# A two-layer hybrid decoder trunk on one core: the first block of the down matrix moved ahead of the last gate and up product, a float32 copy of x made on GpSimd, and constants loaded later

## The chip, the core and the metric

The kernel runs on one core of a Trainium2 chip. A core has TensorE (PE, matrix products into PSUM), VectorE (DVE), ScalarE (ACT), GpSimd (POOL) and SyncE (SP, which issues the large DMAs here). Each engine works through its own instructions in the order in which they stand and waits for the others at semaphores. The metric is the time of one execution on the device in microseconds. The kernel before takes 2764.95 us, the median of three runs (2758.95 to 2766.28).

## The reference

Two layers run over 512 positions of width 1024 in float32. Each layer is a half-step SwiGLU feed-forward network, a mixer of three parallel branches, and a second feed-forward network, with a layer norm behind each:

```
def swiglu(x, w_gate, w_up, w_down):
    return (jax.nn.silu(x @ w_gate) * (x @ w_up)) @ w_down

for l in range(DEPTH):                       # DEPTH = 2
    x = layer_norm(DEEPNORM_ALPHA * x + 0.5 * swiglu(x, ffn1_gate[l], ffn1_up[l], ffn1_down[l]), ln_g[l, 0], ln_b[l, 0])
    mix = token_mixing(x, w_in[l], ...)      # sparse attention, dilated attention, gated MLP; rope tables and masks
    x = layer_norm(DEEPNORM_ALPHA * x + mix, ln_g[l, 1], ln_b[l, 1])
    x = layer_norm(DEEPNORM_ALPHA * x + 0.5 * swiglu(x, ffn2_gate[l], ffn2_up[l], ffn2_down[l]), ln_g[l, 2], ln_b[l, 2])
```

The hidden width is 2816, so gate and up are 1024 x 2816 matrices and down is 2816 x 1024. So there are four feed-forward stages in a run, and the change touches these and nothing in the mixers.

## The kernel before

**Numbers in two parts.** Every operand of TensorE is kept as a high part (rounded to fp32r) and a low part (the rest), and a product is three matmuls: high by high, high by low, low by high (`mm3`, L460 to L462). Making the two parts is a copy on ScalarE and a subtraction on VectorE (or GpSimd). For weights this is `split_w`: L386 the copy into `wh`, L389 the subtraction into `wl`. Weights come by DMA into three `raw` buffers (L424) and are split into eight half buffers, which are handed out again when a product has used them (`put_w`). `pump(look)` splits as many weights ahead as there are free halves.

**Start of a feed-forward stage.** The four row blocks of x (128 positions each) are transposed on TensorE when they are needed (`ensure_x`, `x_transposed`): transposes L534, high part on ScalarE L537, low part on VectorE L540, and a float32 copy `xt` from PSUM on ScalarE L542. From the third block on `x_sums` builds sums of quarters of x out of `xt`: L557 and L559 on VectorE, L558 and L560 on GpSimd, then their two parts (L563, L564). The first two of the 22 column blocks of gate and up are done plainly, first over the positions of blocks 0 and 1, then over those of 2 and 3.

**Gate and up.** For the other 20 blocks (`f`) the product of a 2 x 2 split of x with one of gate and up is done with seven quarter products instead of eight (`A11`, `S1`, `A12`, `S2`, `A22`, `S4`, `S3`; `product`, twelve matmuls of 256 columns each). The sums of weight quarters are made by GpSimd (L407). Results leave PSUM by small copies and additions (L780, L782, L784, L787, L791, L793, L795). `A22` of a block is left for the next block: `end(prev)` runs it behind `S2` of the block that follows, so that it does not have to wait for L795, which reads the same PSUM bank. Behind the last block there is none that follows, and `end(prev)` (L799) comes right behind `S3` and its L795. `product` calls `pump(LOOK)` right behind `put_w`, so the splits of weights stand ahead of the copy out of PSUM on ScalarE and VectorE.

**Down.** `make(n)` splits a 128-row block of the hidden matrix (L808 on ScalarE, L809 on VectorE). Its ten places are taken from an area of 80 blocks (L802), which takes in that of the quarter sums of x, freed behind the last `end` (L800). `tm_gemm` then runs eleven weight blocks for each half of the output columns; a weight block is 24 matmuls of 512 columns, 2 rows of the hidden matrix by 4 row blocks by 3. The first weight block is called block 0 here, and the place where gate and up end and down begins is called the turn.

**Constants.** Rope tables and masks are first used in the mixer. They are loaded by GpSimd's own DMAs in block `f == 4` of the first stage (`load_consts`), and GpSimd turns the masks into bf16 (L509) when they have landed.

## Time and profile before

| | |
|---|---|
| median of three runs | 2764.95 us |
| the profiled execution | 2764.18 us |
| its span, first to last instruction | 2762.5 us |
| TensorE busy | 2630.4 us (95%) |
| VectorE busy | 1769.6 us (64%) |
| ScalarE busy | 1233.1 us (45%) |
| GpSimd busy | 1234.2 us (45%) |
| moved by DMA | 248.72 MB, mean 90 GB/s |

The profiled execution's time lies 1.7 us over its span, and it is 0.8 us under the median. Shares of busy time are means over stages that differ; where a stage is bound is read from the waits of the engine that is never long idle, TensorE. Its busy time holds stretches in which it ran at half its clock, which the page's row PEclk and the stretches below show.

### The profile page before, as it was taken

The page shows a single profiled execution, that of the slowest core. Times are in us where ns is not written, and L with a number is a line of the kernel's source. Part 1 is how long each engine was busy: PE and PEld are TensorE (multiplying, and loading weights), DVE is VectorE, ACT ScalarE, POOL GpSimd, SP SyncE. Part 2 cuts the span into 40 slices and gives each one's busy share as a digit, 9 for nine tenths or more (in the row PEclk, how much of TensorE's full clock was granted, in tenths as well). Part 3 has the DMA queues.
Part 4 walks back from the last instruction along what each step waited for, and adds up shares of the span by engine and source line. Part 5 has one row for each costly group of instructions (what it writes and reads, how often), then busy time and mean ns, then how long its engine had stood idle before and what let it go on. Part 6 is the DMA issues. An engine that isn't in the chain of part 4 may idle for free. (4 is left out here: it accounts for less than half of the span.)

```text
span 2762.5 us, 43188 instructions
## 1 busy us (share of the span) xinstructions
PE 2630.4 (95%) x16446; PEld 2369.3 (86%) x16446; DVE 1769.6 (64%) x3187; ACT 1233.1 (45%) x2442; POOL 1234.2 (45%) x981
## 2 busy tenths in 40 slices
PE   8999999989999999999989999999899999999998
PEld 8998888877788879997889988888777888899977
DVE  7786565557552379884588765655674424788746
ACT  5454334345642235554355543344456422355542
POOL 5663015454655427760067720254446444376500
PEclk9999999999999999999999999999999999999999
DMA  3333223111212332333223333221112123233332
GB/s 137 119 101 115 96 101 99 36 62 47 69 41 90 102 127 93 107 108 101 83 84 101 107 116 96 96 97 51 54 39 76 43 95 117 98 107 108 100 107 77
DMA packets 71216, 248.72 MB, mean 90 GB/s; under 512 B 8016, under 2 KB 10096, under 8 KB 71008
## 3 DMA queue, kind: packets, MB, share of 16 engines
q1 hardware_dynamic: 68832, 238.25, 25.7%
q0 software_dynamic: 2176, 7.71, 0.9%
q8 instruction: 129, 2.11, 0.3%
q14 instruction: 79, 0.65, 0.1%
HBM read 239.64 MB, written 6.29 MB: 89 GB/s over the span
## 5 line engine op out<-in xcount | busy, mean ns | idle before, releaser
L460 PE MATMUL P<-R,wh 128*128 128x256 f32 (+1 forms) x2976 | 905.5, 304 | 44.3 <-DVE Fa L795 17.6
L461 PE MATMUL P<-R,wh 128*128 128x256 f32 (+1 forms) x2976 | 901.5, 303 | 4.4 <-DVE R L540 4.4
L462 PE MATMUL P<-R,wl 128*128 128x256 f32 (+1 forms) x2976 | 900.7, 303 | 0.8 <-POOL wl L389 0.8
L386 ACT CAST wh<-raw 128x1024 fp32r<-128x1024 f32 (+4 forms) x525 | 429.6, 824 | 546.1 <-PE P L462 261.6
L389 POOL TENSOR_TENSOR wl<-raw,wh 128x1024 fp32r<-128x1024 f32 (+4 forms) x159 | 352.2, 2222 | 704.6 <-ACT wh L386 701.1
L460 PEld LDWEIGHTS P<-R,wh 128*128 128x128 f32 x2976 | 576.4, 194 | 69.2 <-DVE Fa L795 18.4
L389 DVE TENSOR_TENSOR wl<-raw,wh 128x512 fp32r<-128x512 f32 (+2 forms) x367 | 402.0, 1098 | 353.3 <-ACT wh L386 352.9
L460 PE MATMUL P<-wh,R 128*128 128x512 f32 (+3 forms) x1600 | 588.0, 367 | 11.9 <-ACT R L808 5.8
L461 PEld LDWEIGHTS P<-R,wh 128*128 128x128 f32 x2976 | 576.8, 194 | 24.5 <-DVE R L540 6.1
L462 PEld LDWEIGHTS P<-R,wl 128*128 128x128 f32 x2976 | 576.8, 194 | 20.5 <-POOL wl L389 1.0
L462 PE MATMUL P<-wh,R 128*128 128x512 f32 (+3 forms) x1600 | 576.8, 360 | 6.1 <-DVE R L540 4.1
L461 PE MATMUL P<-wl,R 128*128 128x512 f32 (+3 forms) x1600 | 576.7, 360 | 4.1 <-POOL wl L389 2.1
L389 DVE TENSOR_TENSOR wl<-Fa,wh 128x512 fp32r<-128x512 f32 x320 | 361.7, 1131 | 117.3 <-ACT wh L386 116.4
L460 PEld LDWEIGHTS P<-wh,R 128*128 128x128 f32 x1600 | 306.4, 191 | 53.0 <-ACT R L808 6.9
L462 PEld LDWEIGHTS P<-wh,R 128*128 128x128 f32 x1600 | 305.9, 191 | 51.3 <-DVE R L540 5.2
L461 PEld LDWEIGHTS P<-wl,R 128*128 128x128 f32 x1600 | 306.9, 192 | 44.4 <-POOL wl L389 2.9
L407 POOL TENSOR_TENSOR Fa<-raw 128x512 f32<-128x512 f32 x160 | 227.7, 1423 | 199.8 <-DMA raw<-in_wts 189.0
L386 ACT CAST wh<-Fa 128x512 fp32r<-128x512 f32 x320 | 197.1, 617 | 158.3 <-PE P L461 85.0
L407 POOL TENSOR_TENSOR Fa<-raw,Fa 128x512 f32<-128x512 f32 x80 | 135.5, 1693 | 1.9 <-DVE wl L389 1.9
L407 POOL TENSOR_TENSOR Fa<-Fa,raw 128x512 f32<-128x512 f32 x80 | 127.5, 1593 | 6.3
L793 ACT ACTIVATE Fa<-Fa 128x512 f32<-128x512 f32 x80 | 50.6, 632 | 154.3 <-DVE Fa L791 154.3
L1635 POOL TENSOR_SCALAR Fa<-Fa,ac,ga 128x128 f32<-128x128 f32 (+3 forms) x128 | 79.3, 630 | 84.1 <-DVE ac L1631 83.7
(222 smaller groups left out, 3151.0 us busy)
## 6 DMA issues: line engine op xcount, KB each, us to landing
raw<-in_wts SPq DMA_DIRECT2D x400, 512.0 KB, 3.3
raw<-in_wts SPq DMA_DIRECT2D x16, 480.0 KB, 3.2
x_sp<-Fa SPq DMA_DIRECT2D x8, 512.0 KB, 5.3
Fa<-x_sp SPq DMA_DIRECT2D x8, 512.0 KB, 5.2
Fa<-in_ln_g POOLq DMA_DIRECT2D x6, 512.0 KB, 5.2
Fa<-in_ln_b POOLq DMA_DIRECT2D x6, 512.0 KB, 5.8
raw<-in_wts SPq DMA_DIRECT2D x8, 320.0 KB, 3.0
Fa<-in_x SPq DMA_DIRECT2D x4, 512.0 KB, 6.4
```

The lines of the kernel that those rows point to most:

```text
L386: nc.scalar.copy(h, r)
L389: (nc.gpsimd if kind == "full" and (self.pool_lo or j == 1) else nc.vector).tensor_tensor(lo, r, hf, op=OP.subtract)
L407: self.nc.gpsimd.tensor_tensor(v, x, y, op=op)
L460: mm(out, lh, rh, start=start, stop=False, skip_group_check=more)
L461: mm(out, lh, rl, start=False, stop=False, skip_group_check=more)
L462: mm(out, ll, rh, start=False, stop=stop, skip_group_check=more)
L793: nc.scalar.activation(st["g"], st["g"], AF.Silu)
L1635: t.nc.gpsimd.tensor_scalar(e, e, rd[:, br:br + 1], t.ga[:, s["i"], c:c + 1], op0=OP.mult, op1=OP.mult)
```

## The change

There are four edits.

1. In `x_transposed` the float32 copy `xt` is no longer copied out of PSUM by ScalarE. GpSimd adds the high and the low part of x, which lie in SBUF, behind the two subtractions of VectorE.
2. `pump(LOOK)` is called behind the copy out of PSUM instead of inside `product`, and not behind `S3` of the last block.
3. The turn: three of the places for split rows of the hidden matrix are taken in a free area before the blocks begin, and the other eight are those of the quarter sums of x. The first three rows are split behind block 20 of gate and up. `end` of the last block is called by `tm_gemm` through `begun`, behind block 0 of down.
4. `load_consts` is called behind that `end` in the first stage.

```diff
--- before.py
+++ after.py
@@ -258,6 +258,7 @@
         self.xh = self.Ra[:, 0:4096].rearrange("p (k t) -> p k t", k=KT)
         self.xl = self.Ra[:, 4096:8192].rearrange("p (k t) -> p k t", k=KT)
         self.xhf = self.Raf[:, 0:4096].rearrange("p (k t) -> p k t", k=KT)
+        self.xlf = self.Raf[:, 4096:8192].rearrange("p (k t) -> p k t", k=KT)
         self.x = self.Fa[:, FB * 128:].rearrange("p (i d) -> p i d", i=NT)
         dram = ctx.enter_context(tc.tile_pool(name="dr", bufs=1, space=bass.MemoryType.DRAM))
         self.x_sp = dram.tile([NT, 128, D], F32, name="x_sp")
@@ -538,9 +539,10 @@
             jobs.append((b, src, ks, ts))
         for b, src, ks, ts in jobs:
             nc.vector.tensor_tensor(self.xl[:, ks, ts], src, self.xhf[:, ks, ts], op=OP.subtract)
-            if ffn:
-                nc.scalar.copy(xt[:, ks, ts], src)
             self.unbank(b)
+        if ffn:
+            for b, src, ks, ts in jobs:
+                nc.gpsimd.tensor_tensor(xt[:, ks, ts], self.xhf[:, ks, ts], self.xlf[:, ks, ts], op=OP.add)
         if spill:
             self.fa.free(FB + i * KT, KT)
         if ffn and i >= 2:
@@ -620,7 +622,7 @@
             self.nc.vector.scalar_tensor_tensor(xs[:, c], xs[:, c], r, b[:, c], op0=OP.mult, op1=OP.add)
 
 
-    def tm_gemm(self, lhs, nk, l, j, last=False, done=lambda k: None):
+    def tm_gemm(self, lhs, nk, l, j, last=False, done=lambda k: None, begun=lambda: None):
 
         pa, g, b = self.ln_params(l, j)
         if j == 0:
@@ -640,6 +642,8 @@
                 self.put_w(w)
                 done(n * 2)
                 done(n * 2 + 1)
+                if h + n == 0:
+                    begun()
             if h == 0:
                 for t in range(NT):
                     self.residual(t, 0, pb[t])
@@ -755,7 +759,6 @@
                 self.mm3(self.P[b][:, :256], wh[:, ks], wl[:, ks], rh[:, k], rl[:, k],
                          k == 0 and not more, k == 3, more)
             self.put_w(w)
-            self.pump(LOOK)
 
         def end(st):
             f, b = st["f"], st["beta"]
@@ -763,8 +766,18 @@
             nc.vector.tensor_tensor(H(f, slice(0, 256)), st["g"][:, :256], self.P[b][:, :256], op=OP.mult)
             self.unbank(b)
             nc.gpsimd.tensor_tensor(H(f, slice(256, 512)), st["g"][:, 256:], st["p"], op=OP.mult)
+            self.pump(LOOK)
             self.fa.free(st["ga"], 4)
             self.fa.free(st["pa"], 2)
+
+        made, used = [0], [0]
+        spare = [self.ra.alloc(8) for _ in range(3)]
+        places = spare + [self.xt_at + n for n in range(0, 64, 8)]
+
+        def make(n):
+            a, v = places[n % len(places)], H(n % NF)
+            self.nc.scalar.copy(self.rv(a, 4), v)
+            self.nc.vector.tensor_tensor(self.rv(a + 4, 4), v, self.rvf(a, 4), op=OP.subtract)
 
         prev = None
         for f in range(PLAIN, NF):
@@ -778,50 +791,54 @@
             P = [self.P[b][:, :256] for b in (beta, gamma, alpha)]
             product(st, A11, beta)
             nc.scalar.copy(g1, P[0])
+            self.pump(LOOK)
             product(st, S1, gamma)
             nc.scalar.copy(p, P[1])
+            self.pump(LOOK)
             product(st, A12, alpha)
             nc.vector.tensor_tensor(g1, P[2], g1, op=OP.add)
             self.unbank(alpha)
+            self.pump(LOOK)
             product(st, S2, beta, True)
             nc.scalar.copy(g2, P[0])
+            self.pump(LOOK)
             if prev:
                 end(prev)
             product(st, S4, gamma, True)
             nc.vector.tensor_tensor(g2, P[1], g2, op=OP.add)
             self.unbank(gamma)
             nc.scalar.activation(st["g"], st["g"], AF.Silu)
+            self.pump(LOOK)
             product(st, S3, beta, True)
             nc.vector.tensor_tensor(p, P[0], p, op=OP.add)
             prev = st
-            if l + j == 0 and f == 4:
-                self.load_consts()
-        end(prev)
-        self.ra.free(self.xt_at, 64)
-
-        base = self.ra.alloc(80)
-        made, used, hs = [0], [0], NT * 2
-
-        def make(n):
-            a = base + n % 10 * 8
-            v = H(n % NF)
-            self.nc.scalar.copy(self.rv(a, 4), v)
-            self.nc.vector.tensor_tensor(self.rv(a + 4, 4), v, self.rvf(a, 4), op=OP.subtract)
+            if f == NF - 2:
+                for n in range(3):
+                    make(n)
+                    made[0] += 1
+            if f < NF - 1:
+                self.pump(LOOK)
 
         def lhs(k):
             n = k if used[0] < NF else NF + k
-            while made[0] < min(max(n + 5, used[0] + 8), used[0] + 10, 2 * NF):
+            while made[0] < min(max(n + 5, used[0] + 8), used[0] + len(places), 2 * NF):
                 make(made[0])
                 made[0] += 1
             assert made[0] > n >= used[0]
-            a = base + n % 10 * 8
+            a = places[n % len(places)]
             return self.rv(a, 4), self.rv(a + 4, 4)
 
         def done(k):
             used[0] += 1
 
-        self.tm_gemm(lhs, NF, l, j, last, done)
-        self.ra.free(base, 80)
+        def begun():
+            end(prev)
+            if l + j == 0:
+                self.load_consts()
+
+        self.tm_gemm(lhs, NF, l, j, last, done, begun)
+        for a in places:
+            self.ra.free(a, 8)
         self.fa.free(more[0][0], (NF - HB // 4) * 4)
```

How the instructions stand. At the end of gate and up, `P7` is the bank of the last block's product and `P4`, `P2`, `P3`, `P1` are those of down. TensorE before goes from the last product (both `S3` and `A22` write P7) to block 0:

```order
L460 MATMUL P7_78<-R_63,wh_69 128x256
L461 MATMUL P7_78<-R_63,wh_69 128x256
L462 MATMUL P7_78<-R_63,wl_70 128x256
L460 MATMUL P4_75<-wh_69,R_63 128x512
L461 MATMUL P4_75<-wl_70,R_63 128x512
L462 MATMUL P4_75<-wh_69,R_63 128x512
```

TensorE now, first the end of `S3` and the begin of block 0, then the end of block 0, `A22` and block 1:

```order
L463 MATMUL P7_78<-R_63,wl_70 128x256
L461 MATMUL P4_75<-wh_69,R_63 128x512
L462 MATMUL P4_75<-wl_70,R_63 128x512
...
L463 MATMUL P1_72<-wh_69,R_63 128x512
L461 MATMUL P7_78<-R_63,wh_69 128x256
L462 MATMUL P7_78<-R_63,wh_69 128x256
L463 MATMUL P7_78<-R_63,wl_70 128x256
...
L463 MATMUL P7_78<-R_63,wl_70 128x256
L461 MATMUL P4_75<-wh_69,R_63 128x512
```

The twelve matmuls of `A22` have moved behind the 24 of block 0.

ScalarE at the same place, before (`wh<-Fa` and `wh<-raw` are splits of weights, 128x512 a quarter and 128x1024 a block of down; `Fa<-P` copies out of PSUM; `R<-H` rows of the hidden matrix):

```order
L793 ACTIVATE Fa<-Fa 128x512
L386 CAST wh<-Fa 128x512
L780 COPY Fa<-P_78 128x256
L782 COPY Fa<-P_76 128x256
L386 CAST wh<-raw 128x1024
L787 COPY Fa<-P_78 128x256
L386 CAST wh<-raw 128x1024
L793 ACTIVATE Fa<-Fa 128x512
L386 CAST wh<-raw 128x1024 x2
L808 CAST R<-H 128x512 x10
```

ScalarE now:

```order
L810 ACTIVATE Fa<-Fa 128x512
L387 CAST wh<-Fa 128x512
L779 CAST R<-H 128x512 x3
L387 CAST wh<-Fa 128x512
L793 COPY Fa<-P_78 128x256
L796 COPY Fa<-P_76 128x256
L387 CAST wh<-raw 128x1024
L803 COPY Fa<-P_78 128x256
L810 ACTIVATE Fa<-Fa 128x512
L387 CAST wh<-raw 128x1024 x2
L779 CAST R<-H 128x512 x5
```

Three splits of the hidden matrix stand a whole block earlier, the last split of a quarter stands behind them, and the second weight block of down is split behind the activation instead of ahead of it.

GpSimd at the start of the second gate and up stage, before (the layer norm's parameters, four subtractions for the first plain weights, the sums of x):

```order
L603 DMA Fa<-in_ln_b 128x1024
L389 TENSOR_TENSOR wl<-raw,wh 128x1024 x4
L558 TENSOR_TENSOR H<-H 128x512
L560 TENSOR_TENSOR H<-H 128x512
L558 TENSOR_TENSOR H<-H 128x512
```

GpSimd now:

```order
L605 DMA Fa<-in_ln_b 128x1024
L545 TENSOR_TENSOR H<-R 128x4x128 x2
L390 TENSOR_TENSOR wl<-raw,wh 128x1024 x3
L545 TENSOR_TENSOR H<-R 128x4x128 x2
L390 TENSOR_TENSOR wl<-raw,wh 128x1024
L545 TENSOR_TENSOR H<-R 128x4x128 x2
L560 TENSOR_TENSOR H<-H 128x512
L562 TENSOR_TENSOR H<-H 128x512
L545 TENSOR_TENSOR H<-R 128x4x128 x2
```

The additions (L545) stand ahead of the subtractions for the first weights and ahead of both sums of x.

## Rows read from the trace of the kernel before

**Rows 1.** The page: busy time by engine, and one group of GpSimd additions.
```profile
PE 2630.4 (95%) x16446; PEld 2369.3 (86%) x16446; DVE 1769.6 (64%) x3187; ACT 1233.1 (45%) x2442; POOL 1234.2 (45%) x981
...
L407 POOL TENSOR_TENSOR Fa<-raw,Fa 128x512 f32<-128x512 f32 x80 | 135.5, 1693 | 1.9 <-DVE wl L389 1.9
```

**Rows 2.** TensorE's waits: waiting line, releaser: us in all, times, longest.
```profile
PE P L460 <- DVE Fa L795: 17.6, 4, 4.4
...
PE P L460 <- ACT Fa L780: 9.1, 11, 1.8
```

**Rows 3.** Timeline of TensorE, first turn: start, us, instruction [idle before <-releaser].
```profile
251.94 0.58 PE L460 MATMUL P<-R,wh 128*128 128x256 f32 x1 [4.41 <-DVE Fa L795]
...
256.31 0.79 PE L460 MATMUL P<-wh,R 128*128 128x512 f32 x1 [1.44 <-ACT R L808]
...
257.98 0.79 PE L462 MATMUL P<-wh,R 128*128 128x512 f32 x1 [0.45 <-DVE R L809]
```

**Rows 4.** Stretches around two turns: us, busy us by engine, PEclk, DMA share, GB/s.
```profile
247.60:262.20 14.60, 8.37 (x27) 6.53 (x28) 9.09 (x15) 7.81 (x13) 2.86 (x5) 0.65 0.50 186
1252.10:1270.00 17.90, 11.60 (x36) 9.05 (x37) 10.30 (x16) 7.81 (x13) 1.79 (x3) 0.62 0.47 147
251.94:260.80 8.86, 6.97 (x21) 5.37 (x22) 5.03 (x8) 6.11 (x11) 2.86 (x5) 0.50 0.66 246
1256.50:1267.80 11.30, 9.40 (x26) 7.26 (x27) 7.47 (x12) 6.25 (x11) 1.79 (x3) 0.50 0.59 186
```

**Rows 5.** Timelines of VectorE and ScalarE, first turn.
```profile
242.81 1.22 DVE L389 TENSOR_TENSOR wl<-raw,wh 128x1024 fp32r<-128x1024 f32 x1 [2.89 <-ACT wh L386]
...
255.64 5.29 ACT L808 CAST R<-H 128x512 fp32r<-128x512 f32 x10
...
257.24 6.10 DVE L809 TENSOR_TENSOR R<-H,R 128x512 fp32r<-128x512 f32 x10
```

**Rows 6.** Timeline and one stretch after the constants are loaded.
```profile
76.46 1.68 POOL L509 CAST masks<-Fa 128x1792 bf16<-128x1792 f32 x1 [6.54 <-DMA Fa<-in_consts]
...
80.34 0.58 PE L460 MATMUL P<-R,wh 128*128 128x256 f32 x1 [2.93 <-ACT Fa L782]
...
80.34:83.40 3.06, 3.06 (x14) 3.06 (x15) 3.06 (x4) 1.81 (x4) 3.06 (x3) 0.50 0.03 3
```

**Rows 7.** Timeline of TensorE, early in the second gate and up stage.
```profile
1074.62 0.39 PE L460 MATMUL P<-R,wh 128*128 128x256 f32 x1 [1.81 <-ACT Fa L780]
```

**Rows 8.** Timelines of four engines, start of the second gate and up stage.
```profile
1011.86 1.28 DVE L540 TENSOR_TENSOR R<-P,R 128x512 fp32r<-128x512 f32 x2
...
1014.80 7.02 POOL L389 TENSOR_TENSOR wl<-raw,wh 128x1024 fp32r<-128x1024 f32 x3 [41.48 <-ACT wh L386]
...
1017.14 0.38 PE L460 MATMUL P<-R,wh 128*128 128x256 f32 x1 [3.14 <-ACT R L537]
...
1027.95 1.28 DVE L540 TENSOR_TENSOR R<-P,R 128x512 fp32r<-128x512 f32 x2
...
1029.29 0.69 DVE L557 TENSOR_TENSOR H<-H 128x512 f32<-128x512 f32 x1
...
1029.93 1.30 POOL L558 TENSOR_TENSOR H<-H 128x512 f32<-128x512 f32 x1 [3.75 <-ACT H L542]
...
1030.08 1.69 DVE L559 TENSOR_TENSOR H<-H 128x512 f32<-128x512 f32 x1
...
1034.07 1.07 ACT L537 CAST R<-P 128x512 fp32r<-128x512 f32 x2
...
1034.70 0.38 PE L460 MATMUL P<-R,wh 128*128 128x256 f32 x1 [1.96 <-ACT R L537]
...
1035.92 0.58 PE L461 MATMUL P<-R,wh 128*128 128x256 f32 x1 [0.83 <-DVE R L540]
```

**Rows 9.** Timelines of GpSimd and VectorE, start of the program.
```profile
5.92 1.04 POOL L388 TENSOR_SCALAR wh<-raw 128x1024 fp32r<-128x1024 f32 x1 [4.28 <-DMA raw<-in_wts]
...
7.34 0.69 DVE L540 TENSOR_TENSOR R<-P,R 128x512 fp32r<-128x512 f32 x1 [0.16 <-ACT R L537]
```

## The prediction

> **What bounds the kernel now.** I read the engines' busy shares first, then TensorE's waits, then the timeline around the longest of them. TensorE is busy 95% of the span and no other engine over 64% [rows 1]. So a change is worth what it takes out of TensorE's waits, or puts in, and a microsecond saved elsewhere is worth nothing by itself. The change leaves the count and size of the matmuls alone. Among the waits, two groups lie in code that the change touches: 17.6 us in four waits for L795, and 9.1 us in eleven waits for L780 [rows 2].
>
> Four times 4.4 us is one wait at each turn. The timeline of the first turn shows three waits in a row [rows 3]: 4.41 us until VectorE has added into p (L795, which holds the bank that `A22` needs), 1.44 us until ScalarE has split the first row of the hidden matrix (L808), which could not begin before `A22` had released its place, and 0.45 us for the low part of it. That is 6.30 us of idle time. The granted clock shows a second price: from 251.94 to 260.80 it is 0.50, the lower of the two levels (1.2 instead of 2.4 GHz), and before it fell TensorE had stood idle [rows 4]. TensorE was busy 6.97 us of that stretch. At full clock this work takes half the time at best; I count 46% of it as lost, since a little of each matmul's spacing does not scale: 3.2 us. A turn thus costs 6.3 + 3.2 = 9.5 us. At the second turn the low clock lasts longer (busy 9.40 us at 0.50, to 1267.80, and a mean of 0.62 instead of 0.65 over the turn [rows 4]), so 6.3 + 4.3 = 10.6 us. The other two look like the first. All four: 3 x 9.5 + 10.6 = 39.1 us.
>
> **Part 1: the turn.** Now block 0 stands between `S3` and `A22`. What it needs is early enough. Its weights' low part is ready at 242.81 + 1.22 = 244.03 [rows 5], 3.6 us before TensorE falls idle at 247.53 (251.94 - 4.41), and that split keeps its place. Its rows 0 and 1 of the hidden matrix are split a block earlier: three copies of 0.53 us (5.29 / 10) and three subtractions of 0.61 us (6.10 / 10) [rows 5], 1.6 and 1.8 us ahead of one quarter's split. A product's length follows from rows 3: `A22` ran from 251.94 to 254.87 (256.31 - 1.44) at half clock, 2.93 us, so some 1.5 us at full clock. Behind the three copies come the last quarter's split, used six products later, and the copy L793, whose bank `S2` wants two products (3 us) after `A11` has ended; 1.6 us more fit into that. I cost them at nothing; if that cover were gone, `S2` would wait up to 1.6 us per stage. While block 0 runs, VectorE does its L795 and `A22` finds its bank free. Block 0 has the columns of four products, so it lasts up to 6 us, against the 4.4 us that were missing. Rows 3 to 7 go into the places of the quarter sums, which were read last by `S3`; five copies take 2.6 us, five subtractions 3.1 us, and block 1 needs only row 3 of them. The addition behind `A22` now stands in VectorE's queue ahead of the split of the fourth weight block, which is wanted three such blocks later. So I expect no wait in place of the old ones, and no fall of the clock: gain 39.1 us. Bounds: 20 (a wait of half the size stays and the clock still falls) to 39.
>
> **Part 2: constants.** At f == 4 GpSimd waits 6.54 us for the masks and then converts them for 1.68 us; the sums for the next quarters stand behind this, ScalarE stands behind the sums, and TensorE waits 2.93 us for a copy that ScalarE has behind them. Then the clock is 0.50 for 3.06 us of full work [rows 6], of which 46% is 1.4 us. All of it goes: 4.3 us. At the new place GpSimd has nothing behind the masks until the second half of down, and the first user of the constants is the mixer; I cost the move at nothing. The cover is that idle time; without it the same 8 us would come at a place where nobody waits.
>
> **Part 3: order of splits and copies.** The waits for L780 (9.1 us) fall in the first blocks of each stage, where VectorE has a backlog of weight splits ahead of its own additions; the longest are 1.81 us [rows 7]. Each copy and addition now stands ahead of one more split. One split less takes 0.69 to 1.69 us off (L557 alone, L559 beside GpSimd, the same shape [rows 8]) where the mean wait is 0.8. The backlog itself stays. I take 3 us, from 0 to 9. In exchange each quarter is split one product later; seven products still lie between, so I cost that at nothing, and at up to 3 us if the first blocks feel it.
>
> **Part 4: the copy on GpSimd.** ScalarE loses 32 copies, GpSimd gains 32 additions. The nearest price is L558 with the same shape, 1.30 us [rows 8]; beside a busy VectorE 1.69 us [rows 1]. At the start of a stage three chains meet them.
> - The first weights. Before, ScalarE's copies stood ahead of the splits of weights, so that TensorE waited 3.14 us and began at 1017.14. Now ScalarE is ready near 1014, but GpSimd does two additions (2.6 us) behind VectorE's L540 (from 1011.86 [rows 8], first half done at 1012.5) before the first weights' low part: 1012.5 + 2.6 + 2.34 (7.02 / 3) = 1017.4. TensorE's third matmul needs it, and before this came two matmuls behind 1017.14, so the two are near level. I take 0.3 us of gain for each of three stages: 0.9 us.
> - The sums of x. L540 of the third block ends at 1029.2; GpSimd's two additions now lie between it and the sums (1028.6 + 2 x 1.30 = 1031.2, where L558 began at 1029.93). Everything behind moves by about 1.4 us: the last split of a sum, ScalarE's L537 for the fourth block at 1034.07, and with it the two waits of TensorE, 1.96 and 0.83 us [rows 8]. That is a loss of 1.4 us, with up to 2 more if the clock stays low for longer: I take 1.8 for each of three stages, 5.4 us.
> - The start of the program. The first weights are copied by GpSimd itself at 5.92; now this stands behind two additions that need VectorE's L540 (first half at 7.2, second from 7.34 [rows 9]): 7.2 + 2.6 = 9.8, so 3.9 us later, some of which TensorE would have spent waiting for x anyway. I take 3.5 us.
> The part costs 3.5 + 5.4 - 0.9 = 8.0 us; from 0 (ScalarE's freed time pays for it) to 16 (1.69 us each, longer low clock).
>
> The Trainium skill, "SBUF — State Buffer", section "SBUF: two separate sides", speaks against this part: VectorE and GpSimd share one pair of ports, and whoever of a GpSimd operation and a VectorE operation with two SBUF inputs comes second is blocked until the first has ended. The trace agrees: L559 takes 1.69 us beside L558 and ends 0.5 us behind it, where L557 alone takes 0.69 us on the same shape [rows 8]. By that rule an addition can cost VectorE its whole length too; this is the rival on the far side below.
>
> **Sum.** 39.1 + 4.3 + 3 - 8.0 = 38.4 us off the profiled execution's 2764.18 gives 2725.8; the median of the runs shown is 0.8 us above that execution, too little to move it. I predict 2726 us.
>
> **Rivals.**
> - A new wait at the turn (the three early copies hold up `S2`, or the second weight block, now split behind the activation, is late for block 1). For: VectorE and ScalarE are the engines on which every step there depends. Against: every margin that I found is over a microsecond. It would leave half of the turn's price: 38.4 - 20 = 18 us, 2746.
> - GpSimd is hidden and the early waits vanish. For: ScalarE's queue was the releaser in most of the waits at the start. 39.1 + 4.3 + 9.1 = 52.5 us, 2712.
> - Slower: the additions in series. All eight of a stage lie on the path, at 1.69 us each and each again as a block on VectorE's backlog in the first blocks: 32 x 1.69 = 54.1 us, and four longer stretches at low clock of 1.6 us: 60.5 against 46.4 us of gain, 2778. It decides from 12 us per stage on. Against: four of the eight lie beside TensorE's work on the first plain blocks.
> - The change does not do what it says: TensorE then falls into the same waits one block later (`A22` behind block 0 waits for L795 all the same), 2764.
>
> **Chances.** Forecast 0.62, half the turn 0.17, more hidden 0.14, slower 0.03, nothing 0.04. The forecast's own range is 2716 to 2738. The range that I give is 2711 to 2747; it holds the second and third case. About 0.3% (8.3 us) is what a measurement of this kernel can tell from no change; faster by more has 0.93, within it 0.04, slower 0.03.
>
> **What would show it.** Right: no wait for L813 (L795 before) at the four turns, TensorE's clock at 1.00 through them, `A22` behind 24 matmuls of 512 columns; no wait of TensorE near 80 us; GpSimd's L545 between L541 and L559, with ScalarE's L538 of the fourth block a good microsecond later against the first matmul of the stage. Wrong: a wait at the turn for L780, L390 or L793; waits of L793 in the first blocks that grow; a TensorE that stands more than 5 us longer at the start of a stage.

## The result, and the profile after

The changed kernel takes 2734.52 us (median of four runs, 2732.04 to 2737.01); the kernel before took 2765.61 us beside it. The ratio is 0.989, with a 95% interval of 0.9869 to 0.9912: 30.4 us faster (30.4 = 0.011 x 2765.6), where 38.4 were forecast. 2726 us were predicted, with a range of 2711 to 2747. The time lies in the range and 8.5 us above the forecast, and that difference is not spread evenly: three terms of the sum were too small, and one that goes the other way was too small by 14.5 us.

Lines have moved: L407 is now L408, L460 to L462 are L461 to L463, L389 L390, L537 and L540 L538 and L541, L780 L793, L787 L803, L795 L813, L808 L779. The additions on GpSimd are L545.

The page's busy line:

```profile
PE 2619.1 (96%) x16446; PEld 2363.4 (86%) x16446; DVE 1813.5 (66%) x3187; ACT 1202.7 (44%) x2410; POOL 1296.7 (47%) x1013
```

ScalarE has 32 instructions less than in [rows 1], GpSimd 32 more, and two additions take 2.53 us (below), the price that was taken from L558. VectorE has the very same 3187 instructions and is busy 43.9 us longer (1813.5 - 1769.6). An engine that takes longer for the same instructions is held up while it works, and such time is in no row of waits. But this is no measure of the loss: in experiment 1, which has no addition on GpSimd and is the faster kernel, VectorE is busy 1797.1 us, so 27.5 of the 43.9 us are there as well. From the first cast of x to the end of the plain blocks, where the loss is, VectorE's busy time grows by 16.4 us over the four stages.

**The turn** is as forecast. Both waits of [rows 2] that belong to it (17.6 us for L795, and those of [rows 3] behind it) have gone. The timeline of the first turn:

```profile
248.35 0.40 PE L461 MATMUL P<-wh,R 128*128 128x512 f32 x1
...
253.82 0.28 PE L461 MATMUL P<-R,wh 128*128 128x256 f32 x1
...
250.38 0.42 DVE L813 TENSOR_TENSOR Fa<-P,Fa 128x256 f32<-128x256 f32 x1
```

Block 0 begins at 248.35 and lasts 5.47 us; `A22` follows at 253.82 without a gap, since VectorE ended its L813 at 250.80. Stretches of 20 us around the first two turns (busy time of PE, PEld, DVE, ACT, POOL, then the clock) answer to [rows 4], and below them stands the stretch at low clock in the start of the second gate and up stage, of which more further down:

```profile
245.00:265.00 20.00, 20.00 (x109) 17.37 (x108) 15.18 (x21) 11.39 (x17) 8.26 (x11) 1.00 0.73 254
1242.00:1262.00 20.00, 20.00 (x111) 17.42 (x110) 15.12 (x21) 11.41 (x18) 2.70 (x3) 1.00 0.59 190
1026.60:1033.40 6.80, 4.59 (x19) 4.30 (x20) 5.91 (x7) 2.21 (x4) 4.29 (x4) 0.50 0.01 2
```

TensorE is busy all of both turns at 1.00, where it had a mean of 0.65 and 0.62. From the Silu of the tenth block of a stage to the first addition of down, the four stages are 9.6, 11.0, 11.1 and 10.5 us shorter in the two profiles: 42.2 us.

**The starts** are where it was lost. From the first cast of x to the end of the plain blocks the four stages are longer by 7.3, 4.5, 5.3 and 5.5 us: 22.5 us, where 8.0 were forecast. TensorE's waits (us in all, times, longest), to be read against [rows 2] and the 3.14, 1.96 and 0.83 us of [rows 8]:

```profile
PE P L461 <- ACT R L538: 16.8, 4, 5.2
...
PE P L463 <- POOL wl L390: 10.2, 4, 3.0
...
PE P L461 <- ACT Fa L793: 6.2, 8, 1.0
```

The rows of one start, of four engines, answer to [rows 8]:

```profile
1004.47 0.28 PE L461 MATMUL P<-R,wh 128*128 128x256 f32 x1
...
1008.16 0.39 PE L463 MATMUL P<-R,wl 128*128 128x256 f32 x1 [3.01 <-POOL wl L390]
...
1028.17 0.58 PE L461 MATMUL P<-R,wh 128*128 128x256 f32 x1 [5.23 <-ACT R L538]
...
1003.28 2.53 POOL L545 TENSOR_TENSOR H<-R 128x512 f32<-128x512 f32 x2 [39.34 <-DVE R L541]
1005.77 7.99 POOL L390 TENSOR_TENSOR wl<-raw,wh 128x1024 fp32r<-128x1024 f32 x3
1013.73 2.52 POOL L545 TENSOR_TENSOR H<-R 128x512 f32<-128x512 f32 x2
1016.22 2.40 POOL L390 TENSOR_TENSOR wl<-raw,wh 128x1024 fp32r<-128x1024 f32 x1
...
1011.26 1.04 ACT L387 CAST wh<-raw 128x1024 fp32r<-128x1024 f32 x1 [6.78 <-DMA raw<-in_wts]
1012.21 0.29 ACT L592 ACTIVATE ac<-ac,eps 128x1 f32<-128x1 f32 x1
...
1027.54 1.06 ACT L538 CAST R<-P 128x512 fp32r<-128x512 f32 x2
...
1004.02 1.29 DVE L541 TENSOR_TENSOR R<-P,R 128x512 fp32r<-128x512 f32 x2 [0.23 <-ACT R L538]
...
1012.53 0.16 DVE L596 RECIPROCAL ac<-ac 128x1 f32<-128x1 f32 x1 [3.34 <-ACT ac L592]
1012.73 1.05 DVE L597 TENSOR_TENSOR ac<-ac 128x1 f32<-128x1 f32 x1
1013.82 1.22 DVE L598 TENSOR_TENSOR ac<-ac 128x1 f32<-128x1 f32 x1
1015.07 1.20 DVE L599 SCALAR_TENSOR_TENSOR ac<-ac 128x1 f32<-128x1 f32 x1
1016.30 3.52 DVE L622 SCALAR_TENSOR_TENSOR Fa<-Fa,ac 128x512 f32<-128x512 f32 x2
1019.75 1.28 DVE L541 TENSOR_TENSOR R<-P,R 128x512 fp32r<-128x512 f32 x2
...
1021.83 1.75 DVE L559 TENSOR_TENSOR H<-H 128x512 f32<-128x512 f32 x1 [0.81 <-POOL H L545]
```

The rows to see are L597 to L599 and L622, which wait for nothing. The first three work on one column and take 1.05 to 1.22 us: L597 ends with the third subtraction for the weights (L390, to 1013.76), L598 and L599 each with one of two additions (to 1016.25). L622 takes 3.52 us for two halves, beside the subtraction for the fourth weight (1016.22 to 1018.62). They belong to the layer norm of x's block 3, which VectorE has ahead of block 2's L541. L596, a reciprocal with one operand, takes 0.16 us beside the same subtraction that L597 has to wait for. L541, which reads PSUM and one operand in SBUF, keeps its 1.29 us for two at 1004.02, in the middle of two other additions.

### The profile page after: what moved, and what is told of

It reads as the page before. It is cut to its first block, busy times and chain, and to the rows that moved or that the text cites. A ratio compares the mean times of both kernels' runs of the same rounds, so it can differ in the third digit from the quotient of the medians.

```text
span 2734.2 us, 43041 instructions
## 1 busy us (share of the span) xinstructions
PE 2619.1 (96%) x16446; PEld 2363.4 (86%) x16446; DVE 1813.5 (66%) x3187; ACT 1202.7 (44%) x2410; POOL 1296.7 (47%) x1013
## 4 chain that ended last, share of the span: by engine, by line
PE 81%; DVE 11%; ACT 3%; POOL 3%; issue 2%; DMA 0%; DVEq 0%; ACTq 0%; POOLq 0%
PE P L461 25%; PE P L463 25%; PE P L462 25%; PE P L1591 1%; PE P L1698 1%; DVE wl L390 1%; POOL wl L390 1%; DVE Fa L622 1%; POOL H L545 1%; PE P L1627 1%; DVE Fa L1525 1%; PE P L1662 1%; PE P L862 1%; DVE R L566 1%; ACT wh L387 1%
## 5 line engine op out<-in xcount | busy, mean ns | idle before, releaser
L461 PE MATMUL P<-R,wh 128*128 128x256 f32 (+1 forms) x2976 | 903.9, 304 | 24.7 <-ACT R L538 16.8
L463 PE MATMUL P<-R,wl 128*128 128x256 f32 (+1 forms) x2976 | 901.3, 303 | 10.3 <-POOL wl L390 10.2
L462 PE MATMUL P<-R,wh 128*128 128x256 f32 (+1 forms) x2976 | 900.6, 303 | 4.1 <-DVE R L541 4.0
L390 DVE TENSOR_TENSOR wl<-raw,wh 128x512 fp32r<-128x512 f32 (+2 forms) x367 | 427.9, 1169 | 295.5 <-ACT wh L387 292.4
L461 PEld LDWEIGHTS P<-R,wh 128*128 128x128 f32 x2976 | 576.2, 194 | 47.1 <-ACT R L538 17.7
L463 PEld LDWEIGHTS P<-R,wl 128*128 128x128 f32 x2976 | 575.9, 194 | 32.0 <-POOL wl L390 10.9
L462 PEld LDWEIGHTS P<-R,wh 128*128 128x128 f32 x2976 | 576.2, 194 | 25.2 <-DVE R L541 6.4
L461 PE MATMUL P<-wh,R 128*128 128x512 f32 (+3 forms) x1600 | 583.6, 365 | 6.5 <-DVE R L869 5.6
L463 PE MATMUL P<-wh,R 128*128 128x512 f32 (+3 forms) x1600 | 573.0, 358 | 4.3 <-DVE R L541 4.1
L462 PE MATMUL P<-wl,R 128*128 128x512 f32 (+3 forms) x1600 | 573.1, 358 | 4.2 <-POOL wl L390 2.1
L390 POOL TENSOR_TENSOR wl<-raw,wh 128x1024 fp32r<-128x1024 f32 (+4 forms) x159 | 354.5, 2236 | 458.8 <-ACT wh L387 458.2
L390 DVE TENSOR_TENSOR wl<-Fa,wh 128x512 fp32r<-128x512 f32 x320 | 366.2, 1145 | 91.8 <-ACT wh L387 91.8
L461 PEld LDWEIGHTS P<-wh,R 128*128 128x128 f32 x1600 | 304.5, 190 | 46.1 <-issue 6.6
L463 PEld LDWEIGHTS P<-wh,R 128*128 128x128 f32 x1600 | 304.0, 190 | 46.4 <-DVE R L541 5.2
L462 PEld LDWEIGHTS P<-wl,R 128*128 128x128 f32 x1600 | 304.5, 190 | 43.6 <-POOL wl L390 2.9
L408 POOL TENSOR_TENSOR Fa<-raw 128x512 f32<-128x512 f32 x160 | 235.6, 1472 | 197.8 <-DMA raw<-in_wts 181.5
L387 ACT CAST wh<-Fa 128x512 fp32r<-128x512 f32 x320 | 190.3, 617 | 5.1 <-POOL Fa L408 5.1
L545 POOL TENSOR_TENSOR H<-R 128x512 f32<-128x512 f32 x32 | 41.4, 1313 | 224.2 <-DVE R L541 224.2
L408 POOL TENSOR_TENSOR Fa<-raw,Fa 128x512 f32<-128x512 f32 x80 | 139.3, 1741 | 1.4 <-DVE wl L390 1.4
L408 POOL TENSOR_TENSOR Fa<-Fa,raw 128x512 f32<-128x512 f32 x80 | 127.8, 1597 | 6.3
```

The source lines that it names most:

```text
L387: nc.scalar.copy(h, r)
L390: (nc.gpsimd if kind == "full" and (self.pool_lo or j == 1) else nc.vector).tensor_tensor(lo, r, hf, op=OP.subtract)
L408: self.nc.gpsimd.tensor_tensor(v, x, y, op=op)
L461: mm(out, lh, rh, start=start, stop=False, skip_group_check=more)
L462: mm(out, lh, rl, start=False, stop=False, skip_group_check=more)
L463: mm(out, ll, rh, start=False, stop=stop, skip_group_check=more)
```

## The experiments

The theory behind the first experiments: the turn, the constants and the order of splits gave more than forecast, and all that is missing was lost at the starts, to the additions on GpSimd and what they block. The rival: the starts lose because TensorE, no longer held up elsewhere, arrives there earlier. Ratios are against the kernel before, run beside each; experiments 1 to 4, 5 to 8 and 9 to 11 were run together, each group on another chip. A difference of two ratios is uncertain by about 0.25% (7 us), so of small terms the profiled stretches are told as well.

| kernel | median us | ratio (95%) |
|---|---|---|
| changed kernel | 2734.5 | 0.9890 (0.9869 to 0.9912) |
| 1: changed, copy on ScalarE | 2711.9 | 0.9798 (0.9785 to 0.9812) |
| 2: before, copy on GpSimd alone | 2791.6 | 1.0087 (1.0073 to 1.0101) |
| 3: before, turn alone | 2725.3 | 0.9847 (0.9834 to 0.9861) |
| 4: changed, constants at f == 4 | 2741.4 | 0.9910 (0.9896 to 0.9924) |
| 5: changed, splits inside products | 2742.8 | 0.9920 (0.9904 to 0.9935) |
| 6: additions for blocks 2, 3 alone | 2726.4 | 0.9865 (0.9844 to 0.9886) |
| 7: additions for blocks 0, 1 alone | 2723.4 | 0.9846 (0.9828 to 0.9865) |
| 8: kernel 1, sums late | 2726.9 | 0.9859 (0.9839 to 0.9879) |
| 9: kernel 1, block 0's copies later | 2705.5 | 0.9769 (0.9756 to 0.9782) |
| 10: kernel 9, one sum's split later | 2700.8 | 0.9759 (0.9745 to 0.9772) |
| 11: changed, one-input operations | 2721.6 | 0.9829 (0.9816 to 0.9843) |

**1. Part 4 undone.**

```
             nc.vector.tensor_tensor(self.xl[:, ks, ts], src, self.xhf[:, ks, ts], op=OP.subtract)
+            if ffn:
+                nc.scalar.copy(xt[:, ks, ts], src)
             self.unbank(b)
-        if ffn:
-            for b, src, ks, ts in jobs:
-                nc.gpsimd.tensor_tensor(xt[:, ks, ts], self.xhf[:, ks, ts], self.xlf[:, ks, ts], op=OP.add)
```

> The changed kernel with part 4 alone undone: x's float32 copy is made by ScalarE from PSUM again; the turn, the constants and the order of splits stay as changed. Theory (the starts of the four gate/up stages lost 22.5 us in the changed kernel, and the additions on GpSimd are the whole cause): that comes back, 2734.5 - 22.5 = 2712 us (2709 to 2716), and TensorE's wait before the last transposed block of x is 1.96 us again, not 5.2. Rival A (the starts lose because the work that the turn and the new order move lets TensorE arrive there earlier, and the additions cost only the 8 us that were forecast): 2726 us, with waits of 3 to 4 us left at the starts. Rival B (the additions cost nothing): 2734 us.

2711.9 us; against the changed kernel 0.92% or 25 us. The theory holds, and this kernel is faster than both. Its rows for the same start, with the numbers of the chain:

```profile
1015.64 0.39 PE L461 MATMUL P<-R,wh 128*128 128x256 f32 x1 [1.80 <-ACT R L538]
...
1004.74 2.38 POOL L390 TENSOR_TENSOR wl<-raw,wh 128x1024 fp32r<-128x1024 f32 x1 [1.84 <-ACT wh L387]
...
1004.56 0.29 ACT L591 ACTIVATE ac<-ac,eps 128x1 f32<-128x1 f32 x1
...
1015.01 1.07 ACT L538 CAST R<-P 128x512 fp32r<-128x512 f32 x2
...
1005.08 2.05 DVE L596 TENSOR_TENSOR ac<-ac 128x1 f32<-128x1 f32 x1
...
1007.56 1.42 DVE L621 SCALAR_TENSOR_TENSOR Fa<-Fa,ac 128x512 f32<-128x512 f32 x2
1008.89 1.28 DVE L541 TENSOR_TENSOR R<-P,R 128x512 fp32r<-128x512 f32 x2
...
1010.23 0.69 DVE L558 TENSOR_TENSOR H<-H 128x512 f32<-128x512 f32 x1
```

Between the square root of block 3's norm and the first cast of block 3, the two kernels now differ step by step. Square root to block 2's L541: 4.33 us here (1008.89 - 1004.56), 7.54 in the changed kernel (1019.75 - 1012.21), so 3.2 more. Of these the three one-column operations are 1.1 us (3.47 in sum against 2.37, since here one of them pays too, beside the subtraction at 1004.74), and the norm's last step on 512 columns is 2.1 us (L622 with 3.52 against 1.42): there the fourth weight's subtraction, which block 1's additions pushed back, stands beside it. L541 to the first subtraction for the sums: 1.34 and 2.08, 0.7 more; this is the wait for block 2's additions. From that subtraction to the cast of block 3: 4.78 and 5.71, 0.9 more, about what the stretched L559 takes beyond 0.69 us. Ahead of the square root the changed kernel is 1.9 us quicker, counted from the first cast of x (12.87 us against 14.78): the fourth weight's split, which waits for its DMA ahead of the root on ScalarE, comes that much earlier, with no copies of x on this engine. What of it is the copies' doing was not taken apart. The sum is +3.0 us, and the plain blocks behind it take 1.7 us more, at a clock that stays at the lower level for 6.80 us (the stretch above), and here for half of that: 4.7 us for this stage. The stretch in this kernel:

```profile
1016.60:1020.00 3.40, 3.14 (x14) 3.14 (x15) 3.24 (x5) 1.83 (x4) 1.28 (x1) 0.51 0.02 5
```

**2. Part 4 alone**, in the kernel before (the diff of experiment 1 the other way round).

> The kernel before with part 4 alone: x's float32 copy on GpSimd. Theory (the cost lies in GpSimd's additions and in what they block on VectorE, whatever else is changed): the starts lose about 22.5 us and nothing else moves, 2765.6 + 22.5 = 2788 us (2783 to 2792). Rival A (the cost comes only together with the other parts): 2765.6 + 8 = 2774 us or less. Rival B: level, 2766 us.

2791.6 us, 0.87% or 24 us slower than before, as the theory had it. The four starts lose 7.2, 4.5, 5.2 and 5.5 us in its profile, within 0.1 us of what they lose with the other parts. TensorE's wait at the same place:

```profile
1042.39 0.58 PE L461 MATMUL P<-R,wh 128*128 128x256 f32 x1 [4.08 <-ACT R L538]
```

So the loss belongs to part 4 and does not depend on when TensorE arrives. Alone, part 4 makes the kernel slower by more than a measurement's uncertainty.

**3. The turn alone**, in the kernel before: the diff of the change without the additions, the moved `pump` calls and the moved `load_consts`.

> The kernel before with the turn alone: block 0 of down ahead of the last product, three rows of the hidden matrix split early; the copy on ScalarE, constants at f == 4, splits inside the products. Theory (the turn gave 42 us by itself): 2765.6 - 42 = 2723.5 us (2720 to 2727), TensorE without a wait at the four turns, the wait of 2.9 us near 80 us still there. Rival (part of the turn's gain needs the additions to stand ahead of the splits, part 3): a wait of 1 to 2 us for VectorE stays at each turn with a low clock behind it, some 2740 us.

2725.3 us: 1.53% or 42 us. The profile has no wait at the four turns, and from the tenth Silu to the first addition of down the stages are 10.4, 11.3, 9.7 and 10.6 us shorter. The wait near 80 us is still there, as expected, with 3.47 us. The rival falls.

**4. The constants back at f == 4**, all else as changed.

```
+            if l + j == 0 and f == 4:
+                self.load_consts()
             if f < NF - 1:
                 self.pump(LOOK)
...
         def begun():
             end(prev)
-            if l + j == 0:
-                self.load_consts()
```

> The changed kernel with the constants loaded at f == 4 again, all else as changed. Theory (the late load gave the 4.3 us that were forecast): 2734.5 + 4.3 = 2739 us (2737 to 2741), with TensorE's wait of about 3 us near 80 us back. Rival (with the copies ahead of the splits ScalarE's backlog no longer reaches TensorE there): level, 2734 to 2735 us, no wait near 80 us.

2741.4 us, 0.20% or 5.5 us by the ratios, which are uncertain by more; in the profiles the first stage is 6.1 us longer from its plain blocks to the tenth Silu, and the other three are level within 0.9. Neither the theory's wait of 3 us near 80 us nor the rival's none: GpSimd waits 6.21 us for the masks as in [rows 6], and TensorE pays in two smaller waits, without a fall of the clock:

```profile
83.48 1.68 POOL L510 CAST masks<-Fa 128x1792 bf16<-128x1792 f32 x1 [6.21 <-DMA Fa<-in_consts]
...
87.90 0.39 PE L461 MATMUL P<-R,wh 128*128 128x256 f32 x1 [1.69 <-ACT Fa L803]
95.21 0.39 PE L461 MATMUL P<-R,wh 128*128 128x256 f32 x1 [1.30 <-ACT Fa L793]
```

**5. Part 3 undone:** `pump(LOOK)` stands inside `product` again, ahead of the copy or addition behind it.

```
             self.put_w(w)
+            self.pump(LOOK)
...
             nc.scalar.copy(g1, P[0])
-            self.pump(LOOK)
             product(st, S1, gamma)
             nc.scalar.copy(p, P[1])
-            self.pump(LOOK)
```

> The changed kernel with part 3 alone undone: the splits are issued inside a product again, ahead of the copy or addition behind it. Theory (the forecast's term): 2734.5 + 3 = 2737.5 us (2735 to 2739). Rival (the difference of two earlier runs: the changed kernel with the copy on ScalarE against the turn alone, 2711.9 against 2725.3, less 0.20% or 5.5 us for the constants): 2734.5 + 7.8 = 2742 us (2740 to 2744), with three or four waits of TensorE for ScalarE's copies in the first blocks of each stage and with waits in the last blocks ahead of the turn.

2742.8 us, 0.30% or 8.3 us: the rival's value, though the waits that it expected ahead of the turn are not there (none from a stage's 18th Silu on). In the profile the stretch from the plain blocks to the first addition of down is 5.7 us longer over the four stages, and the waits for L793 are 10.5 us instead of 6.2:

```profile
PE P L461 <- ACT Fa L793: 10.5, 11, 1.9
```

Between 5.7 and 8.3 us the size of the term is not settled.

**6 and 7. The additions for half of the blocks.** The edit, against the changed kernel; where it is not on GpSimd, the copy is ScalarE's:

```
+            if ffn and i < 2:                # experiment 7: i >= 2
+                nc.scalar.copy(xt[:, ks, ts], src)
             self.unbank(b)
-        if ffn:
+        if ffn and not i < 2:
```

> The changed kernel with the copies of x's blocks 0 and 1 on ScalarE again and the additions on GpSimd for blocks 2 and 3 alone. Base: all copies on ScalarE, 2711.9 us. Theory (the loss at a start has two places: the additions of block 1 and the weights' subtractions that they push back stand beside the norm of block 3 and stretch VectorE there by 3.2 us; the additions of block 2 keep VectorE waiting 0.7 us and stretch one of its subtractions by about 1 us): here only the second place is left, with the three one-column operations of the norm at the length they have with all copies on ScalarE (2.37 us for the three, against 3.47 us in the changed kernel), and the casts of block 3 come 1.7 us later: 1.7 to 3 us a stage, 2719 to 2724 us. Rival (all of the loss is that the first weights' low part waits for the additions of block 0): 2712 us.

> The changed kernel with the additions on GpSimd for x's blocks 0 and 1 alone; blocks 2 and 3 are copied by ScalarE. Theory (two places, as for the other half): the norm of block 3 is stretched by 3.2 us and ScalarE's freed time gives 1.9 us back, so the casts of block 3 come 1.3 us later, 1.3 to 2.6 us a stage in three stages; the start of the program, where the first weights' copy stands behind the additions, loses about 5 us of its 7.3: 2711.9 + 9 to 13 = 2721 to 2725 us, with VectorE's first subtraction for the sums back at 0.69 us. Rival (all of the loss comes from the first weights' low part behind the additions of block 0): the whole 22.5 us stay, 2734 us. Rival on the other side (the additions of blocks 0 and 1 are hidden): 2712 us or less, since TensorE's wait for ScalarE at the second block goes.

2726.4 and 2723.4 us; the theory had 2719 to 2724 and 2721 to 2725. VectorE's rows separate the two places, as it said. With the additions for blocks 2 and 3 alone, the norm is as with all copies on ScalarE, and the subtraction behind it is stretched:

```profile
1014.57 2.05 DVE L599 TENSOR_TENSOR ac<-ac 128x1 f32<-128x1 f32 x1
1016.65 0.16 DVE L600 TENSOR_TENSOR ac<-ac 128x1 f32<-128x1 f32 x1
...
1020.47 1.76 DVE L561 TENSOR_TENSOR H<-H 128x512 f32<-128x512 f32 x1 [0.81 <-POOL H L547]
```

With the additions for blocks 0 and 1 alone it is the other way round:

```profile
1011.82 0.90 DVE L599 TENSOR_TENSOR ac<-ac 128x1 f32<-128x1 f32 x1
1012.75 1.22 DVE L600 TENSOR_TENSOR ac<-ac 128x1 f32<-128x1 f32 x1
...
1020.07 0.69 DVE L561 TENSOR_TENSOR H<-H 128x512 f32<-128x512 f32 x1
```

In the profiles the starts lose 14 us in the first and 10 us in the second against experiment 1, which together (24.6 us) are near the 23.1 us that both lose at once. The norm's last step goes with the first place as well: 3.52 us with the additions for blocks 0 and 1, 1.42 with those for blocks 2 and 3. The rivals (all at the first weights, or nothing) fall. The first kernel's median is 2.4 us above the upper end expected: a start loses 3.0 to 4.1 us there, not 1.7 to 3, and 1.7 us of it come behind block 3's cast, as in the changed kernel.

**8. Sums late**, with all copies on ScalarE.

```
-        if ffn and i >= 2:
-            self.x_sums(i - 2)
+        if ffn and i == 3:
+            self.x_sums(0)
+            self.x_sums(1)
```

> The changed kernel with all copies on ScalarE (2711.9 us), and the sums of x for blocks 0 and 2 issued behind the casts and subtractions of block 3, not ahead of them. Theory (what sets the end of a start is the order of the queues: block 3's casts stand on ScalarE behind four casts of sums, whose last waits for VectorE and GpSimd in turn): the casts of block 3 follow their transposes at once, TensorE's waits of 1.96 and 0.83 us go, and the low clock behind them in part: 2 to 3.3 us a stage, 2699 to 2704 us. Rival (block 3's casts wait for its transposes or its norm anyway): 2710 to 2712 us. Rival on the other side (the sums come too late for the first products that read them): a wait of 2 to 4 us there per stage, 2715 to 2725 us.

2726.9 us: a miss, 0.61% or 17 us slower than experiment 1 by the ratios, 16 us at the starts in the profiles. The wait for block 3's cast went down to 0.24 us as the theory wanted, and came back with interest:

```profile
1036.99 0.38 PE L463 MATMUL P<-R,wl 128*128 128x256 f32 x1 [3.42 <-DVE wl L390]
```

VectorE had all twelve operations of the sums ahead of the low part of the first quarters' weights, having stood idle 4.88 us for block 3 shortly before. The rival on the far side is right in kind; it named the products that read the sums, and it was the weights behind them in VectorE's queue.

**9 and 10. ScalarE's queue in a better order**, from experiment 1. In 9 the two copies of block 0 are issued behind block 1's casts; in 10 the split of the last sum of blocks 0 and 2 stands behind block 3's subtractions as well.

```
             if ffn:
-                nc.scalar.copy(xt[:, ks, ts], src)
-            self.unbank(b)
+                self.copies.append((b, src, ks, ts))
+            else:
+                self.unbank(b)
+        if ffn and i == 3:                   # experiment 10 only
+            self.t3(3)
+        if ffn and i:
+            for b, src, ks, ts in self.copies:
+                nc.scalar.copy(xt[:, ks, ts], src)
+                self.unbank(b)
+            self.copies = []
...
-        for n in range(4):
+        for n in range(3 if j == 0 else 4):  # experiment 10 only; t3 is the body
```

> All copies of x on ScalarE (2711.9 us as it stands), but the two of block 0 are issued behind the casts of block 1, and hold their banks until then. Theory (TensorE's wait of 3.2 us for ScalarE at the first matmul of a gate/up stage is ScalarE's queue alone: the copies of block 0 wait 2.83 us for VectorE, and three splits of weights and block 1's casts stand behind them): ScalarE splits the weights at once, block 1's casts follow their transposes, the wait falls to about 1 us, with less low clock behind it: 2.5 to 4 us in each of three stages, 2700 to 2704 us. Rival A (the first weights' low part or VectorE's subtraction for block 1 is as late): a wait of about 3 us for one of these in its place, 2710 to 2713 us. Rival B, the other side (the norm of block 3, whose square root stands on ScalarE behind the fourth weight's split, comes later): 2714 us and more.

> As the kernel with block 0's copies behind block 1's casts, and the split of the last of the four sums for blocks 0 and 2 issued behind the casts and subtractions of block 3 (only this one, where an earlier run moved all four sums and VectorE then had their work ahead of the first quarters' weights). Theory: block 3's casts no longer wait for VectorE and GpSimd in turn; TensorE's waits of 1.0 to 1.9 us there fall by about 1 us in each of four stages, 3 to 6 us below the other kernel of this call. Rival (VectorE falls behind by the moved split, and the first quarters' weights are late as when all sums were moved): a wait of VectorE's split of weights near 15 us behind block 3's casts, level with the other kernel or up to 6 us above it.

2705.5 us for 9: the theory's direction, short of its 2700 to 2704, for rival A is partly right. The wait at the first matmuls is 1.84 us, for VectorE's subtraction, no longer 3.17 for ScalarE:

```profile
998.98 0.39 PE L462 MATMUL P<-R,wh 128*128 128x256 f32 x1 [1.84 <-DVE R L541]
```

2700.8 us for 10. The median is 4.7 us lower, as expected, but the two intervals overlap, and in the profiles the four starts are only 0.8 us shorter together: that 10 beats 9 is not shown. Its waits of the same start say why, since VectorE's subtraction takes over from ScalarE's cast:

```profile
996.41 0.38 PE L462 MATMUL P<-R,wh 128*128 128x256 f32 x1 [1.85 <-DVE R L541]
...
1011.63 0.39 PE L462 MATMUL P<-R,wh 128*128 128x256 f32 x1 [1.21 <-DVE R L541]
```

With a ratio of 0.9759 it is 2.4% faster than before and 1.3% faster than the changed kernel, and its clock stays at 1.00 through this start:

```profile
985.00:1025.00 40.00, 36.70 (x274) 34.56 (x273) 38.67 (x51) 22.80 (x38) 23.82 (x12) 1.00 0.20 64
```

**11. One-input operations in place of the additions**, in the changed kernel.

```
-                nc.gpsimd.tensor_tensor(xt[:, ks, ts], self.xhf[:, ks, ts], self.xlf[:, ks, ts], op=OP.add)
+                for n in range(2):
+                    nc.gpsimd.tensor_scalar(xt[:, ks, ts], self.xhf[:, ks, ts], 1.0, 1.0, op0=OP.mult, op1=OP.mult)
```

> The changed kernel with each of GpSimd's additions replaced by two multiplications by one with a single input, the high part of x, into the same place: the copy lacks x's low part. GpSimd's queue is as full, by the 1.04 us that a multiplication of 1024 columns took (two of 512: about 1.0 to 1.3 us for one addition of 1.30). Theory (VectorE's stretched operations come from the use of the memory ports by GpSimd's operations with two inputs): beside these the three one-column operations of block 3's norm take about 0.16 us each, or are stretched only where GpSimd subtracts for the weights, its first subtraction for the sums takes 0.69 us, and the starts lose only the queue's share, some 3 us each: 2720 to 2726 us. Rival A (any operation on GpSimd stretches VectorE's alike): the norm is as long as in the changed kernel, 3.4 us for the three, 2732 to 2737 us. Rival B (single-input operations with this pattern are slow on GpSimd, 1 us or more each): 2740 us and more.

2721.6 us, in the theory's range, but the rows give rival A its due:

```profile
998.86 8.51 POOL L390 TENSOR_TENSOR wl<-raw,wh 128x1024 fp32r<-128x1024 f32 x3
1007.34 0.62 POOL L546 TENSOR_SCALAR H<-R 128x512 f32<-128x512 f32 x1
...
1006.05 0.29 ACT L593 ACTIVATE ac<-ac,eps 128x1 f32<-128x1 f32 x1
...
1006.57 0.82 DVE L598 TENSOR_TENSOR ac<-ac 128x1 f32<-128x1 f32 x1
1007.42 0.54 DVE L599 TENSOR_TENSOR ac<-ac 128x1 f32<-128x1 f32 x1
1008.00 0.16 DVE L600 SCALAR_TENSOR_TENSOR ac<-ac 128x1 f32<-128x1 f32 x1
...
1010.14 1.28 DVE L541 TENSOR_TENSOR R<-P,R 128x512 fp32r<-128x512 f32 x2
```

L599 ends with the first one-input operation, at 1007.96, so it is held beside an operation with one input too, by about 0.4 us; L598's 0.82 us end with the last of the weights' subtractions ahead (1007.37), and L600 is not held. An operation of one input and 512 columns takes GpSimd 0.62 us here, or up to 1.05 beside the norm's last step, instead of 1.26. The rows fit a price that is what is left of the single GpSimd instruction that a VectorE operation meets. From the square root to block 2's L541 this kernel takes 4.09 us (1010.14 - 1006.05), no more than with all copies on ScalarE (4.33), though GpSimd is busy for longer in sum. But the order has moved as well: the fourth weight's subtraction begins at 1010.66, behind the norm, and holds none of it. That it is the second input that makes the difference is not shown. By the ratios part 4 in this form costs 0.31% or 8.6 us: near the 8.0 us that the forecast had for GpSimd's queue, which is all that it had counted. That the two agree is chance in part: against experiment 1 the four starts lose 5.2, 0.6, 1.5 and 1.5 us, where the forecast had 3.5 for the first and 1.5 for each of the others.

## Why the prediction was right, and where not

The forecast holds in the turn, its largest term, and in the direction of each part. That the time lies only 8.5 us from it is partly luck: three gains were 7 to 10 us larger than forecast (3.1, 1.2 and 2.7 to 5.3), and this made up for about half or more of the 14.5 us by which the loss was under-sized.

- **The turn** (39.1 forecast): right in every step. 42.2 us in the profiles, 42 us alone. No wait for L813, nothing in its place, clock at 1.00, `A22` behind 24 matmuls of 512 columns. The three early copies, costed at nothing, cost nothing: `S2` does not wait. Where the 3 us beyond the forecast come from was not taken apart; the share of the low clock is the term that was estimated. One margin was misread: 247.53 - 244.03 is 3.5 us, not 3.6, which changes nothing.
- **Constants** (4.3): 5.5 us by the ratios, which are uncertain by more than the difference. The chain is as told (GpSimd 6.2 us for the masks, then ScalarE, then TensorE); how TensorE pays depends on the order of splits.
- **Order of splits and copies** (3, from 0 to 9): under-sized; 5.7 us in the profiled stretches, 8.3 by the ratios. The step "One split less takes 0.69 to 1.69 us off", against a mean wait of 0.8, took only waits of the kernel before into account. Those for L780 went from 9.1 to 6.2 us, 2.9 as forecast; undone in the changed kernel, the same edit moves them by 4.3.
- **First weights** (a gain of 0.9): right. TensorE waits 3.01 us for GpSimd, where it waited 3.14 and 0.34 us for ScalarE and VectorE [rows 8].
- **The sums of x** (5.4): this is the step that failed. "Everything behind moves by about 1.4 us" counts GpSimd's queue between block 2's L541 and the sums. That share is there (0.7 us of wait), and by its own figures it is 1.3 us (1031.2 - 1029.93). Missing is the block before it: block 1's additions, and the weights' subtractions that they push back, stand beside the layer norm of block 3, which VectorE must finish before block 2's L541. It costs 3.2 us, 1.1 of it in the one-column operations and 2.1 in the norm's last step, and the stretched L559 another 0.9. The prediction had the rule for it and the row that shows it, L559 at 1.69 us, and put it on the far side as a rival that needs "VectorE's backlog in the first blocks". It never asked which VectorE operations stand beside the moved additions. The norm's rows would have shown the price: as L596 in experiment 1, the same operation (L595) takes 2.05 us in the kernel before, beside one of GpSimd's subtractions, and its two neighbours 0.16 us. The prediction's own sign, the fourth block's L538 "a good microsecond later against the first matmul of the stage", came out as 6.1 us (1027.54 - 1004.47 against 1034.07 - 1017.14): 2.8 of it is the cast, 3.3 that the first matmul comes earlier, ahead of the wait for L390. And three of the four starts are over 5 us longer, which it had named as a sign of being wrong, if that is meant of the whole stretch and not of one wait.
- **The start of the program** (3.5): 7.3 us. Up to the first weights the waits of 0.82, 1.28 and 1.13 us stand against one of 0.81, so 2.4 us more; the sums were counted "for each of three stages", and the first stage has them too: its wait for block 3's cast grows from 0.37 to 2.07 us, and the plain blocks behind it, which now have 3.4 us at the lower clock, take 1.7 us more. The last 1.5 us were not taken apart.

The Trainium skill, "SBUF — State Buffer", section "SBUF: two separate sides", says that the shared pair of ports is an exclusive lock for the whole of an instruction, and names VectorE operations with two SBUF inputs. The rows agree: L559, L622 and the one-column L597 to L599 (two operands in SBUF) are held up to the end of the GpSimd instruction beside them, L541 (one in PSUM) beside L545 and L596 (one operand) beside L390 are not. What no run here takes apart is the lock from another cause that would hold the same operations.

What part 4 relieves, ScalarE ahead of the square root, is worth 1.9 us a stage at most. The order of ScalarE's queue was worth more than its load: experiment 9 moves two copies on ScalarE itself, and the starts of the last three stages are 3.1 to 3.9 us shorter than in experiment 1.

## What to carry to other kernels

Before work is moved to GpSimd, list what VectorE does at that time and charge each of its operations that reads two SBUF operands, however few columns it has, with up to one whole GpSimd instruction; a chain of such operations, as in a layer norm, pays that several times over. The instructions that the moved work pushes back in GpSimd's queue count too: here the largest part, 2.1 us, was paid beside one of these. A busy engine ahead of a wait is first tried with another order of its own queue. And an engine whose busy time grows at an unchanged count of instructions is being held up in a way that no row of waits shows; whether that costs anything is read at the place where it grows.

## What the runs showed of the hardware

A VectorE operation on one column with two operands in SBUF, 0.16 us alone, ended in these rows with the GpSimd instruction beside it: it took 1.22 and 1.20 us beside additions of 512 columns (1.26 us each), 1.05 us beside the rest of a subtraction of 1024 columns, and 2.05 us beside nearly a whole one (2.38 us). What is left of the neighbour decided, not the operation's own width. A reciprocal with one operand took 0.16 us in the same place. Two in a row did not share one neighbour but met the next one each, so in this chain the engines took turns. VectorE thus lost over 3 us to its neighbour within one short chain, with the same instructions and without a wait in its rows.
